# Second block's expert weights: two neighbouring whole rows per partition and transfer, in place of half rows 128 rows apart

## The chip, the cores and the metric

One core of a Trainium2 chip runs the kernel. The metric is the device time of one execution in microseconds (us), as the median of three runs: 2299.51 us before (2298.75 to 2302.57). The profile is of one execution of its own, whose span from the first to the last instruction is 2296.6 us, 2.9 us under that median. Engines are named as in the profile: PE (matrix products), PEld (its weight loads), DVE, ACT and POOL (elementwise work), SP (which issues all DMAs here; SPq is its queue).

## The reference, cut to what matters

The program is two transformer blocks over 256 tokens of width 1024. The second block has two layers: layer 0 is a state-space (SSD) mixer and then experts, over the context's 256 tokens and x's 256; layer 1 is attention and then experts, over x alone. In both, each of 16 experts picks its 32 tokens of a sample by router affinity, and all matrices are 1024 x 1024 in float32:

```
for each sample (layer 0: context and x; layer 1: x)
  h    = rmsnorm(x, norm2_w) * (1 + scale) + shift          # by the sample's modulation
  aff  = softmax(h @ router)                                # [256, 16]
  for each expert e: its 32 tokens of largest aff[:, e]
    g   = h[tokens]                                         # [32, 1024]
    y_e = (silu(g @ w1[e]) * (g @ w3[e])) @ w2[e]
    out[tokens] += aff[tokens, e] * y_e
x += gate * out
```

The experts of one layer have 16 x 3 matrices of 4 MB, 201.3 MB; both layers 402.7 MB of the 601.9 MB that the kernel's DMAs move.

## The kernel before

**Groups.** `choice_run` goes through the experts in groups that fill the 128 partitions with their slots: in layer 0 an expert has S = 64 slots (32 of each sample) and a group has EG = 2 experts, 8 groups; in layer 1 S = 32, EG = 4, 4 groups. `choice_group` multiplies a group's gathered rows with w1, w3 and w2. The rows are the stationary operand, S columns wide, and the weights the moving one, 512 columns at a time, so the experts of a group take different column groups of the PE's array (`tile_position=(0, j * S)`): two of them in layer 0, four in layer 1. The contraction over 1024 has 8 chunks, k = 0 to 7.

**Weights.** `choice_tile` (L1635) loads 2 MB into the next slot of a ring: for all EG experts a part of the chunks and one half n of the columns. Partition p holds row k * 128 + p of chunk k, 512 columns of it, so one contiguous run is 2 KB. A layer-0 tile is two DMAs of 1 MB, a layer-1 tile four of 512 KB. Each layer has 96 tiles, 12 per group in layer 0 and 24 in layer 1. A slot is loaded anew when the products that read it are done. All DMAs stand in SP's one queue in program order, and each waits for the completion of the one eight places before it, so at most eight are under way.

**A group's work.** Per half n of the columns: products with w1 and w3 (L1773), tanh (L1804), two DVE products (L1805, L1806), four transposes (L1809) and a copy into actT (L1810). Then per half n of w2's columns: its product (L1773), y in two parts (ACT L1815, DVE L1816), products with `back` that put the slots' rows back to their tokens (L1822, one pair per sample and 128 tokens), times the gate row (`o`, L1825), added to x or ctx (L1826, on DVE and POOL in turn).

**Before the groups.** `choice` loads the router's weights `wr` (L1652) and scales them. `choice_route` (once for each sample) picks the tokens, and gathers their rows by one-hot products (L1741) whose eight outputs, one per chunk k, are scaled and shifted by `mod_cols` columns into `xg` (DVE L1747 and ACT). In layer 0 the route of the context stands between the two `ssd_out` calls. The rows of scale and shift come from `ada_part` (L1201 to L1227), which also stores the gate rows to DRAM.

**Order.** A scheduler orders each engine's instructions; what limits it are the buffers: PSUM tags "p" and "y" of two banks each, "b" of two, single buffers for `y`, `act` and `o`.

Of the kernel before, what the change touches and what calls it, by code (L numbers as in the profile page):

```python
# [18 lines left out]
F32 = mybir.dt.float32  # L19
# [3 lines left out]
AF = mybir.ActivationFunctionType  # L23
OP = mybir.AluOpType
AX = mybir.AxisListType
PSUM = bass.MemoryType.PSUM
# [52 lines left out]
class Net:  # L79
# [30 lines left out]
    def ring(self):  # L110
        """the next weight slot: the lasting ring and a phase's own in turn"""
# [13 lines left out]
    def weight_slots(self, n, side=None):  # L125
        """n more slots for weights, used in turn with those there are"""
# [38 lines left out]
    def columns(self, groups):  # L165
        """vectors over features, turned into one value per partition"""
# [31 lines left out]
    def load_more(self):  # L198
# [4 lines left out]
        # vectors laid out in every partition  # L203
# [25 lines left out]
    def rstd(self, ss, n, width):  # L229
        """(ss / width + EPS) ** -0.5 for [P, n]"""  # L230
# [16 lines left out]
    def norm_rows(self, xs, A4, rs=None):  # L247
        """rows scaled to unit mean square (no gain): one tile per 128 rows"""
# [13 lines left out]
    def norm_halves(self, xs, tile_, rs=None):  # L262
        """the same in tiles of 128 rows' halves; row tile i's chunk k"""
# [19 lines left out]
    def to_features(self, rows, g, hT, t0=0):  # L283
        """hT[:, k, t0:] = gain * transposed rows"""
# [17 lines left out]
    def rope(self, o, x, cg, sg, tmp, twice=None):  # L302
        """o = x * cg + swapped halves of x * sg; [P, 2, heads, d] with tables [P, 2, d]"""
# [14 lines left out]
    def twice(self, o, x, y, op):  # L318
        """o [P, 2, heads, 2, d]: x op y, twice"""
# [4 lines left out]
    def head_rms(self, x, sq, width):  # L324
        """x [P, 2, heads, width] scaled by its heads' rstd; sq a scratch of its shape"""
# [37 lines left out]
    def gained(self, g, d0, d, step, name):  # L363
        """tables of rope with the gain g of its dims in it"""
# [29 lines left out]
    def attend(self, PT, L, v_of, o_ps, shared):  # L394
        """o_ps [P = (parity, 64), heads / 2, P] from weights L [P, heads, nk]"""
# [89 lines left out]
    def wpairs(self, how, pieces, K, c):  # L485
        """a weight in pairs of its K chunks of 128 rows: [P, 2, c] each"""
# [14 lines left out]
    def split_w(self, how, w):  # L501
        """a pair of a weight's chunks, split: for each chunk its hi and lo"""
# [10 lines left out]
    def lin3(self, how, w, hT):  # L513
        """rows of h times w: one PSUM tile per 128 rows"""
# [9 lines left out]
    def feat3(self, how, w, hT, done):  # L524
        """w^T h, feature-major, two chunks of 128 outputs per PSUM tile: done(chunk, psum)"""
# [11 lines left out]
    def mixer(self, keep, tile_, pool):  # L537
# [23 lines left out]
        # indexer  # L561
# [11 lines left out]
        # latent projections  # L573
# [8 lines left out]
        # queries of the attention over the chosen keys  # L582
# [56 lines left out]
        # gates: tanh of half the logits  # L639
# [8 lines left out]
        # the merge, feature-major: 2 * merged  # L648
# [37 lines left out]
    def index_mask(self, i, s):  # L686
        """0 for the 64 highest scores among the keys that a query sees, NEG for the others"""
# [9 lines left out]
    def latent_heads(self, h0, cT, kpe, tile_, M):  # L697
        """queries, keys (turned) and values of four heads"""
# [66 lines left out]
    def padded_keys(self, tile_, k, cT, sT, tag):  # L765
        """one key head, turned: kT[:, 0] has it in partitions 0:64, kT[:, 1] in 64:128"""
# [14 lines left out]
    def pairs_T(self, A4, q):  # L781
        """[P, 2, 2n heads, 64] -> [P = (parity, 64), n, T]"""
# [13 lines left out]
    def memory_keys(self, keep, M, G):  # L796
        """two pieces of work that wait for nothing: the memory's keys (turned) and values"""
# [43 lines left out]
    def memory_read(self, keep, pool):  # L841
# [3 lines left out]
        # queries, feature-major; the norm's gain is in their weights, its rstd with their own in the logits  # L845
# [76 lines left out]
    def raw_features(self, x, junk, put):  # L922
        """both 128 rows of x, turned: put(where, psum); the rstd of their norm"""
# [15 lines left out]
    CAP = 64  # L939

    def group_moe(self, pool, tile_, late):
# [20 lines left out]
        # group: softmax, first of the largest  # L962
# [19 lines left out]
        # experts of the group: the two largest of affinity + bias  # L982
# [22 lines left out]
        # place of a token in its expert's queue  # L1005
# [5 lines left out]
        # 1000 for a token that isn't there  # L1011
# [15 lines left out]
        # the context's rows will be normalised next  # L1027
# [9 lines left out]
    def group_weights(self, what):  # L1037
        """of a pair of experts half of the rows of gate and up, or all of down"""
# [15 lines left out]
    def down_half(self, late, pr, n):  # L1054
        """half of the columns of a pair of experts' down"""
# [6 lines left out]
    def group_round(self, r, ahead, tile_, late, hi, lo, pos, comb):  # L1062
        """tokens whose place in their expert's queue is in CAP * r + [0, CAP)"""
# [104 lines left out]
    def ada_setup(self):  # L1168
# [9 lines left out]
        self.gates = [self.dp.tile([2, 2, D], F32, name=f"gates{l}") for l in range(2)]  # L1178
        self.ada_done = [0, 0]
        self.ada_rows = {}  # L1180

    def ada_step(self, l, n=1):
        """n 48ths of layer l's modulation: each from 128 of the features a sixth of its columns"""
# [8 lines left out]
    def ada_part(self, l):  # L1192
# [32 lines left out]
        if g % 3 == 2:  # L1225
            for r in range(2):
                nc.sync.dma_start(self.gates[l][g // 3, r].rearrange("(j c) -> j c", j=4), rows[r::32, :])  # L1227
# [7 lines left out]
    def mod_cols(self, l, which, r):  # L1235
        """per feature: norm_w * (1 + scale), shift"""
# [7 lines left out]
    def to_features_mod(self, rows, m, sh, hT, t0, tmp=None):  # L1244
        """hT[:, k, t0:] = m * transposed rows + sh; with tmp, hT is a pair of which the sum is that"""
# [22 lines left out]
    def split(self, hi, lo, x, eng=None):  # L1268
        """x = hi + lo, each in float32r"""
# [3 lines left out]
    def mm3(self, p, L, R, start, stop, **kw):  # L1273
        """p += L^T R of split operands (all but the product of the two small parts)"""
# [42 lines left out]
    def ssd_steps(self, tile_, tmp_, A4, hT):  # L1317
        """step sizes and the cumulative sums of the decays; directions and heads over the partitions"""
# [41 lines left out]
        # from here on each of a direction's heads in four of the partitions  # L1360
# [10 lines left out]
        for d in range(2):  # L1371
# [11 lines left out]
            # moving side: cumulative sums of a quarter of the heads  # L1383
# [13 lines left out]
            # stationary side  # L1397
# [13 lines left out]
            # weights of the context's tokens in the state it leaves  # L1411
# [10 lines left out]
            # sums from x's first (or last) token on  # L1422
# [13 lines left out]
    def ssd_project(self, g, pt_, xt_, hT):  # L1436
        """a group's four heads, B and C, all convolved, and the gate; feature-major"""
# [59 lines left out]
    def ssd_group(self, g, xs, BT, CT, zz, tile_, last=None):  # L1497
# [22 lines left out]
        for q in range(2):  # L1520
# [30 lines left out]
        # the context's final states, and what they give x's tokens  # L1551
# [37 lines left out]
    def ssd_out(self, q, tile_):  # L1589
        """the context's tokens (q = 0) or x's"""  # L1590
# [32 lines left out]
    def ssd_rstd(self):  # L1623
        """of the gated rows, from their squares' sums by partition"""
# [10 lines left out]
    def choice_tile(self, nm, l, e0, EG, q, n):  # L1635
# [472 lines left out]
```

## Time and profile before

| | before |
| --- | --- |
| device time, median of 3 | 2299.51 us |
| profiled execution, span | 2296.6 us |
| PE busy | 1981.3 us, 86% |
| DVE, ACT, POOL busy | 42%, 28%, 20% |
| DMA queue q1 | 601.86 MB in 339294 packets, 73.7% of 16 engines |
| matmuls of the experts (L1773), all three forms of 512 columns in the page | 772 us busy |
| last expert weights landed | 2281.17 us |

The page's slices (40 of 57.4 us) show how full each stage is; the chain of waits shows what ended last. PE's busy time counts records that overlap only once, and its share says nothing of which engine a stage waits for: that is read from the waits of the stage.

### The profile page before, as it was taken

How to read it: one execution, taken by the hardware profiler on the slowest of the kernel's cores; microseconds unless marked ns; L12 is line 12 of the kernel's file. 1: busy time of each engine (PE TensorE's matmuls, PEld its weight loads, DVE VectorE, ACT ScalarE, POOL GpSimd, SP SyncE). 2: the span in 40 equal slices, each digit the busy share in tenths (PEclk: the TensorE clock that was granted, in tenths of full speed). 3: DMA queues.
4: the chain of work that ended last, by engine and by line, in shares of the span. 5: the costliest groups of instructions: out<-in, count | busy, mean ns of one | idle time of the engine just before them, and what ended most of it. 6: DMA issues, size and time to landing. Idle time of an engine off the chain costs nothing. (4 is left out here: it accounts for less than half of the span.)

```text
span 2296.6 us, 24819 instructions
## 1 busy us (share of the span) xinstructions
PE 1981.3 (86%) x9384; PEld 1019.8 (44%) x9384; DVE 966.7 (42%) x1675; ACT 637.2 (28%) x1174; POOL 449.2 (20%) x487
## 2 busy tenths in 40 slices
PE   8889878889999999898898888887988788888886
PEld 7667633366776677565332222222755311111111
DVE  6875532268776677665312222223675210100101
ACT  6454422254554455443100000002453000000000
POOL 4430110032242232511101011112652000000000
PEclk9999989989999999999999999999999799999999
DMA  7554849823332322474999999998349899999997
GB/s 235 186 189 142 286 143 346 287 79 111 120 117 95 110 83 84 150 245 174 363 386 387 386 386 387 387 387 331 149 165 329 299 386 387 386 387 387 387 387 280
DMA packets 339421, 603.53 MB, mean 263 GB/s; under 512 B 23611, under 2 KB 97118, under 8 KB 339294
## 3 DMA queue, kind: packets, MB, share of 16 engines
q1 hardware_dynamic: 339294, 601.86, 73.7%
q8 instruction: 76, 1.25, 0.2%
q14 instruction: 51, 0.42, 0.1%
HBM read 597.05 MB, written 4.75 MB: 262 GB/s over the span
## 5 line engine op out<-in xcount | busy, mean ns | idle before, releaser
L1773 PE MATMUL ps<-w,xg 128*64 128x512 f32 (+1 forms) x2048 | 506.1, 611 | 95.2 <-DMA w<-in_moe_w_dram 95.1
L1773 PEld LDWEIGHTS ps<-w,xg 128*64 128x64 f32 (+1 forms) x2048 | 128.1, 124 | 445.6 <-DMA w<-in_moe_w_dram 267.3
L1826 POOL TENSOR_TENSOR x<-x,o 128x512 f32<-128x512 f32 x24 | 39.2, 1635 | 695.1 <-DVE o L1825 695.1
L1276 PE MATMUL ps<-hT,ws 128*128 128x512 f32 x384 | 162.3, 423 | 4.1 <-DVE ada L1215 4.1
L1773 PE MATMUL ps<-w,ctx 128*32 128x512 f32 x512 | 139.5, 608 | 25.6 <-DMA w<-in_moe_w_dram 25.6
L1278 PE MATMUL ps<-hT,ws 128*128 128x512 f32 x384 | 156.1, 406 | 0.0
L1277 PE MATMUL ps<-hT,ws 128*128 128x512 f32 x384 | 155.8, 406 | 0.0
L1773 PE MATMUL ps<-w,actT 128*64 128x512 f32 x512 | 126.7, 599 | 10.7 <-DMA w<-in_moe_w_dram 9.8
L1805 DVE SCALAR_TENSOR_TENSOR act<-act,ps 128x512 f32<-128x512 f32 x24 | 16.5, 687 | 252.6 <-ACT act L1804 252.6
L1806 DVE TENSOR_TENSOR act<-act,ps 128x512 f32<-128x512 f32 x24 | 16.5, 688 | 250.4 <-PE ps L1773 249.7
L1816 DVE SCALAR_TENSOR_TENSOR y<-ps,s,y 128x512 fp32r<-128x512 f32 x24 | 18.0, 750 | 227.7 <-ACT y L1815 227.7
L1481 DVE SCALAR_TENSOR_TENSOR conv<-pad,cols,conv 128x512 f32<-128x512 f32 x124 | 103.6, 836 | 2.4 <-ACT conv L1474 0.2
L1815 ACT ACTIVATE y<-ps,s 128x512 fp32r<-128x512 f32 x24 | 16.5, 687 | 290.1 <-PE ps L1773 271.8
L1276 PEld LDWEIGHTS ps<-hT,ws 128*128 128x128 f32 x384 | 74.3, 193 | 24.5 <-DVE ada L1215 5.3
L1773 PEld LDWEIGHTS ps<-w,ctx 128*32 128x32 f32 x512 | 25.4, 109 | 130.4 <-DMA w<-in_moe_w_dram 102.2
L1278 PEld LDWEIGHTS ps<-hT,ws 128*128 128x128 f32 x384 | 73.9, 192 | 17.4 <-issue 0.4
L1277 PEld LDWEIGHTS ps<-hT,ws 128*128 128x128 f32 x384 | 74.0, 193 | 16.2 <-issue 0.4
L1804 ACT ACTIVATE act<-ps 128x512 f32<-128x512 f32 x24 | 14.3, 597 | 234.6 <-PE ps L1773 232.9
L1773 PEld LDWEIGHTS ps<-w,actT 128*64 128x64 f32 x512 | 37.6, 136 | 79.9 <-issue 61.9
L1271 DVE TENSOR_TENSOR ws<-wr,ws 128x1024 fp32r<-128x1024 f32 x48 | 61.8, 1290 | 26.2 <-ACT ws L1270 17.9
L1822 PE MATMUL ps<-y,back 128*128 128x512 f32 x160 | 58.2, 450 | 16.6 <-ACT y L1815 7.5
L1271 DVE TENSOR_TENSOR ws<-w,ws 128x1024 fp32r<-128x1024 f32 x46 | 61.3, 1338 | 21.8 <-ACT ws L1270 21.6
(632 smaller groups left out, 3754.3 us busy)
## 6 DMA issues: line engine op xcount, KB each, us to landing
w<-in_moe_w_dram SPq DMA_DIRECT2D x192, 1024.0 KB
w<-in_moe_w_dram SPq DMA_DIRECT2D x384, 512.0 KB
adaw<-in_ada_w_dram SPq DMA_DIRECT2D x34, 512.0 KB
w<-in_moe_w_up_dram SPq DMA_DIRECT2D x32, 512.0 KB
w<-in_moe_w_gate_dram SPq DMA_DIRECT2D x32, 512.0 KB
w<-in_moe_w_down_dram SPq DMA_DIRECT2D x16, 1024.0 KB
wr<-in_ssd_in_w_dram SPq DMA_DIRECT2D x16, 1024.0 KB
w<-in_ssd_out_w_dram SPq DMA_DIRECT2D x32, 512.0 KB
```

Of the source, the lines that this page charges most:

```text
L1271: (eng or self.nc.vector).tensor_tensor(lo, x, hi.bitcast(F32), op=OP.subtract)
L1276: t.matmul(p, lhsT=L[0], rhs=R[0], start=start, stop=False, **kw)
L1277: t.matmul(p, lhsT=L[0], rhs=R[1], start=False, stop=False, **kw)
L1278: t.matmul(p, lhsT=L[1], rhs=R[0], start=False, stop=stop, **kw)
L1481: nc.vector.scalar_tensor_tensor(seq(cv), pad[:, :, j:j + 256], tap(j), seq(cv), op0=OP.mult, op1=OP.add)
L1773: nc.tensor.matmul(p[j * S:(j + 1) * S], lhsT=x(k, j), rhs=w[:, j, kk], start=(k == 0), stop=(k == 7), tile_position=(0, j * S))
L1805: nc.vector.scalar_tensor_tensor(act, act, 1.0, pg[0], op0=OP.add, op1=OP.mult)
L1806: nc.vector.tensor_tensor(act, act, pg[1], op=OP.mult)
L1815: nc.scalar.activation(y[:, 0], p, AF.Copy, scale=ws)
L1816: nc.vector.scalar_tensor_tensor(y[:, 1], p, ws, y[:, 0].bitcast(F32), op0=OP.mult, op1=OP.subtract)
L1822: nc.tensor.matmul(q, lhsT=back[:, (2 * s + i) * P:(2 * s + i + 1) * P], rhs=y[:, v], start=(v == 0), stop=(v == 1))
L1826: (nc.gpsimd if i else nc.vector).tensor_tensor(xx[:, i, c], xx[:, i, c], o, op=OP.add)
```

## The change

A tile is now two experts, two chunks and all 1024 columns. The contraction's chunks are dealt out by steps of eight: chunk k is the rows k, 8 + k, 16 + k and so on, so partition p has row 8p + k, and the two chunks of a tile are the rows 8p + 2q and 8p + 2q + 1, one run of 8 KB, 32 KB from the next partition's. All tiles are two DMAs of 1 MB, in layer 1 too, where a group's four experts need two tiles for each q. A product then makes both halves of the columns at once, in two PSUM banks; `act` is one tile of 1024 columns, and the transposes take every eighth column of it (L1829), as the gather does of the rows (L1754). So y, the products with `back` (L1840) and the additions of a group all come after the whole of w2.

The columns of scale and shift must follow the same dealing. `choice_cols` (L1645) loads them with three small DMAs of 32-byte runs for each sample, from norm2_w and from rows that `ada_part` now stores to DRAM as well (`shifts`), into what `wr` no longer needs, and one DVE instruction (L1651) joins them. The final norm's row, loaded into `ctx_x[:, 0]`, comes later, since that place now holds actT for every group of layer 1.

```diff
-    def choice_tile(self, nm, l, e0, EG, q, n):
-        K = 8 // EG
-        v = self.ring().rearrange("p (e k c) -> p e k c", e=EG, k=K)
-        for e in range(EG):
-            src = self.a[nm][l, e0 + e, q * K * P:(q + 1) * K * P, n * 512:(n + 1) * 512]
-            self.nc.sync.dma_start(v[:, e], src.rearrange("(k p) c -> p k c", p=P))
+    def choice_tile(self, nm, l, e0, q):
+        v = self.ring().rearrange("p (e k c) -> p e k c", e=2, k=2)
+        for e in range(2):
+            src = self.a[nm][l, e0 + e].rearrange("(p k) c -> p k c", k=8)
+            self.nc.sync.dma_start(v[:, e], src[:, 2 * q:2 * q + 2])
         return v
+
+    def choice_cols(self, l, r, t):
+        nc = self.nc
+        rows = [self.a["norm2_w_2"][l], self.shifts[l][1, r], self.shifts[l][0, r]]
+        for j, src in enumerate(rows):
+            nc.sync.dma_start(t[:, j], src.rearrange("(p k) -> p k", k=8))
+        nc.vector.scalar_tensor_tensor(t[:, 0], t[:, 1], 1.0, t[:, 0], op0=OP.add, op1=OP.mult)
+        return t[:, 0], t[:, 2]
...
-                nc.tensor.matmul(p, lhsT=v[:, i, k * P:(k + 1) * P],
+                nc.tensor.matmul(p, lhsT=v[:, i, k::8],
...
-        def product(p, nm, n, x):
-            for q in range(EG):
-                w = self.choice_tile(nm, l, e0, EG, q, n)
-                for kk in range(K):
-                    k = q * K + kk
-                    for j in range(EG):
-                        nc.tensor.matmul(p[j * S:(j + 1) * S], lhsT=x(k, j), rhs=w[:, j, kk],
-                                         start=(k == 0), stop=(k == 7), tile_position=(0, j * S))
+        def product(nm, x):
+            tag = self.turn("py")
+            ps = [self.ps(tag) for _ in range(2)]
+            for q in range(4):
+                ws = [self.choice_tile(nm, l, e0 + j, q) for j in range(0, EG, 2)]
+                for k in (2 * q, 2 * q + 1):
+                    for n, p in enumerate(ps):
+                        for j in range(EG):
+                            nc.tensor.matmul(p[j * S:(j + 1) * S], lhsT=x(k, j),
+                                             rhs=ws[j // 2][:, j % 2, k % 2, n * 512:(n + 1) * 512],
+                                             start=(k == 0), stop=(k == 7), tile_position=(0, j * S))
+            return ps
...
-                nc.tensor.transpose(t[:, k], act[:, k * P:(k + 1) * P], self.ident)
+                nc.tensor.transpose(t[:, k], whole[:, 4 * n + k::8], self.ident)
```

PE, layer 0, from one group's w3 to its w2, before (`xg` is the gathered rows, `w` a ring tile, `oc` the next group's one-hot columns; 64x512 is one product into 64 partitions):

```order
L1773 MATMUL ps_11976<-w_11977,xg_10330 64x512 x8
L1773 MATMUL ps_11976<-w_11988,xg_10330 64x512 x8
L1773 MATMUL ps_12009<-w_12010,actT_11876 64x512
L1809 MATMUL ps_12003<-const,act_11999 128x128 x4
L1789 MATMUL ps_12120<-const,oc_12110 128x128 x4
L1773 MATMUL ps_12009<-w_12010,actT_11876 64x512 x7
```

The same place now, from the last tile of w3 on:

```order
L1792 MATMUL ps_11956<-w_11991,xg_10336 64x512
L1792 MATMUL ps_11957<-w_11991,xg_10336 64x512
L1792 MATMUL ps_11956<-w_11991,xg_10336 64x512
L1792 MATMUL ps_11957<-w_11991,xg_10336 64x512
L1792 MATMUL ps_11956<-w_11991,xg_10336 64x512 x2
L1792 MATMUL ps_11957<-w_11991,xg_10336 64x512 x2
L1829 MATMUL ps_12004<-const,act_11885 128x128 x4
L1829 MATMUL ps_12010<-const,act_11885 128x128 x4
L1792 MATMUL ps_12016<-w_12018,actT_11884 64x512
```

A tile's eight products now alternate between two PSUM banks; in the first chunk the two that stand next to each other are the two halves of the same expert, that is of one column group. All eight transposes stand together between w3 and w2.

SP, layer 0, in the second half of `ssd_out`'s weights for x's tokens, before (`w` from in_ssd_out_w, `yd` the mixer's stored output, `g` gate rows, in_moe_w_2 the first expert tile):

```order
L1652 DMA wr_10333<-in_moe_router_w_dram 128x8x16
L1232 DMA g_2219_10335<-gates_348 128x1024
L1232 DMA g_2220_10337<-gates_348 128x1024
L1606 DMA w_10584<-in_ssd_out_w_dram 128x2x512
L1641 DMA w_11430<-in_moe_w_2_dram 128x4x512
L1606 DMA w_10602<-in_ssd_out_w_dram 128x2x512
L1598 DMA y_10925<-yd_6654 128x2x256
L1606 DMA w_10626<-in_ssd_out_w_dram 128x2x512
```

And now:

```order
L1662 DMA wr_10339<-in_moe_router_w_dram 128x8x16
L1234 DMA g_2219_10341<-gates_348 128x1024
L1234 DMA g_2220_10343<-gates_348 128x1024
L1608 DMA w_10598<-in_ssd_out_w_dram 128x2x512
L1642 DMA w_11442<-in_moe_w_2_dram 128x2048
L1608 DMA w_10616<-in_ssd_out_w_dram 128x2x512
L1650 DMA wr_10339<-in_norm_w_dram 128x8
L1650 DMA wr_10339<-shifts_350 128x8 x2
L1650 DMA wr_10339<-in_norm_w_dram 128x8
L1650 DMA wr_10339<-shifts_350 128x8 x2
L1608 DMA w_10640<-in_ssd_out_w_dram 128x2x512
```

The six small DMAs of `choice_cols` stand between two weight loads of `ssd_out`.

DVE, layer 1, after attention (`t` is attention's output times the gate row, ctx the transposed rows for the router):

```order
L2034 TENSOR_TENSOR t_14774<-ps_14706,g_14701 128x512
L2034 TENSOR_TENSOR t_14845<-ps_14779,g_14701 128x512
L1651 SCALAR_TENSOR_TENSOR wr_14680<-wr_14680 128x8
L2034 TENSOR_TENSOR t_14848<-ps_14780,g_14701 128x512
L1705 COPY ctx<-ps_14869 128x4x128
```

The joining instruction stands ahead of the last of four such products (L2016 before).

## Rows read from the trace of the kernel before

**Rows 1.** The page: GB/s of 40 slices, then packets.

```profile
GB/s 235 186 189 142 286 143 346 287 79 111 120 117 95 110 83 84 150 245 174 363 386 387 386 386 387 387 387 331 149 165 329 299 386 387 386 387 387 387 387 280
DMA packets 339421, 603.53 MB, mean 263 GB/s; under 512 B 23611, under 2 KB 97118, under 8 KB 339294
```

**Rows 2.** Windows: length, busy by engine, PEclk, DMA share, GB/s.

```profile
1245.00:1505.00 260.00, 215.38 (x876) 72.14 (x874) 56.78 (x102) 17.80 (x32) 25.21 (x19) 0.99 1.05 386
2000.00:2200.00 200.00, 168.61 (x620) 32.52 (x619) 15.92 (x24) 6.59 (x13) 6.60 (x4) 1.00 1.05 387
```

**Rows 3.** Chain that ended last, layer 1: start, us, what.

```profile
1742.12 9.37 DMA wr<-in_moe_router_w_dram
...
1797.90 9.38 DMA w<-in_moe_w_dram
...
2062.11 10.82 DMA w<-in_moe_w_dram
...
2281.17 1.92 PE ps L1773 x10
```

**Rows 4.** DMA view of 335:340, 395:400, 1300:1500 and 1645:1650.

```profile
DMA packets 1730, 1.76 MB, mean 351 GB/s; under 512 B 54, under 2 KB 1718, under 8 KB 1729
...
DMA packets 572, 2.02 MB, mean 404 GB/s; under 512 B 27, under 2 KB 96, under 8 KB 572
...
DMA packets 38879, 77.30 MB, mean 387 GB/s; under 512 B 1181, under 2 KB 1181, under 8 KB 38871
...
DMA packets 519, 2.07 MB, mean 414 GB/s; under 512 B 15, under 2 KB 15, under 8 KB 518
```

**Rows 5.** PE's waits in 1245:1505: total us, times, longest.

```profile
PE ps L1773 <- DMA w<-in_moe_w_dram: 32.4, 24, 1.6
PE ps L1809 <- DVE act L1806: 5.1, 8, 0.8
PE ps L1822 <- DVE act L1825: 4.4, 8, 0.6
PE ps L1822 <- ACT y L1815: 2.3, 4, 0.6
```

**Rows 6.** PE's timeline, layer 0: start, us, what, idle before.

```profile
1356.82 3.85 PE L1773 MATMUL ps<-w,xg 128*64 128x512 f32 x16 [1.64 <-DMA w<-in_moe_w_dram]
...
1370.47 0.61 PE L1773 MATMUL ps<-w,actT 128*64 128x512 f32 x1
1370.72 0.59 PE L1773 MATMUL ps<-w,xg 128*64 128x512 f32 x1
```

**Rows 7.** PE's timeline, layer 1.

```profile
1791.79 1.92 PE L1773 MATMUL ps<-w,xg 128*32 128x512 f32 x16
```

**Rows 8.** Timeline at the end of layer 0's experts.

```profile
1589.96 0.69 ACT L1815 ACTIVATE y<-ps,s 128x512 fp32r<-128x512 f32 x1 [0.78 <-PE ps L1773]
1590.68 0.75 DVE L1816 SCALAR_TENSOR_TENSOR y<-ps,s,y 128x512 fp32r<-128x512 f32 x1 [3.61 <-ACT y L1815]
...
1595.86 1.64 POOL L1826 TENSOR_TENSOR ctx<-ctx,o 128x512 f32<-128x512 f32 x1 [0.81 <-DVE o L1825]
```

**Rows 9.** Timeline at the kernel's end.

```profile
2283.18 0.69 ACT L1815 ACTIVATE y<-ps,s 128x512 fp32r<-128x512 f32 x1 [16.00 <-PE ps L1773]
2289.19 1.28 DVE L2024 SCALAR_TENSOR_TENSOR x<-x,s,ctx 128x1024 f32<-128x1024 f32 x1 [0.74 <-POOL s L235]
```

**Rows 10.** SP's timeline around `choice`, layer 0.

```profile
970.41 6.72 SPq L1606 DMA_DIRECT2D w<-in_ssd_out_w_dram  x2
```

**Rows 11.** DVE's timeline around `choice`, layer 1.

```profile
1751.51 0.39 DVE L1659 TENSOR_TENSOR mw<-wr,mod 128x128 f32<-128x128 f32 x1 [8.99 <-DMA wr<-in_moe_router_w_dram]
...
1766.84 0.69 DVE L2016 TENSOR_TENSOR t<-ps,g 128x512 f32<-128x512 f32 x1 [4.75 <-PE ps L1278]
```

**Rows 12.** Chain that ended last, at layer 1's gather.

```profile
1793.71 1.12 PE ps L1741 x4
```

**Rows 13.** The page's groups: weight loads of 128 columns (busy, mean ns, idle before).

```profile
L1276 PEld LDWEIGHTS ps<-hT,ws 128*128 128x128 f32 x384 | 74.3, 193 | 24.5 <-DVE ada L1215 5.3
```

More of the change, by code (lines that the diff above doesn't have):

```diff
@@ L1178, in ada_setup @@
         self.gates = [self.dp.tile([2, 2, D], F32, name=f"gates{l}") for l in range(2)]
+        self.shifts = [self.dp.tile([2, 2, D], F32, name=f"shifts{l}") for l in range(2)]
         self.ada_done = [0, 0]
@@ L1224, in ada_part @@
             nc.vector.tensor_copy(o, tv[:, :, :, r].rearrange("p b j -> p j b"))
-        if g % 3 == 2:
+        if g >= 2:
+            to = self.gates[l][g // 3] if g % 3 == 2 else self.shifts[l][g - 3]
             for r in range(2):
-                nc.sync.dma_start(self.gates[l][g // 3, r].rearrange("(j c) -> j c", j=4), rows[r::32, :])
+                nc.sync.dma_start(to[r].rearrange("(j c) -> j c", j=4), rows[r::32, :])
     def gate_row(self, pool, l, gi, r, tag, bufs, tile_=None):
@@ L1666, in choice @@
             o["cw"].append(cw)
+        left = wr.rearrange("p k e -> p (k e)")
+        for s, (_, r) in enumerate(samples):
+            o["cols"].append(self.choice_cols(l, r, left[:, 24 * s:24 * s + 24].rearrange("p (j k) -> p j k", j=3)))
         return o
@@ L1687, in choice_route @@
         aff, pos, xg, mw, cw = o["aff"], o["pos"], o["xg"], o["mw"][s], o["cw"][s]
-        m, sh = self.mod_cols(l, 1, r)
+        m, sh = o["cols"][s]
         hi, lo = tmp_([P, 2, D], "hi", 1, F32R), tmp_([P, 2, D], "lo", 1, F32R)
@@ L1752, in choice_run @@
         for grp in range(16 * S // P):
-            t = actT[:, grp % 2].rearrange("p (k c) -> p k c", k=8) if actT is not None else tile_([P, 8, P], "actT", 2)
-            self.choice_group(o["l"], grp, P // S, S, o["samples"], o["xg"], o["aff"], o["pos"], o["gr"], t, tile_)
+            if actT is None:
+                t, act = tile_([P, 8, P], "actT", 1), tile_([P, D], "act", 1)
+            else:
+                t, act = actT[:, 0].rearrange("p (k c) -> p k c", k=8), actT[:, 1]
+            self.choice_group(o["l"], grp, P // S, S, o["samples"], o["xg"], o["aff"], o["pos"], o["gr"], t, act, tile_)
     def turn(self, tags):
@@ L1759, in turn, with choice_group @@
         return tags[self.turns % len(tags)]
-    def choice_group(self, l, grp, EG, S, samples, xg, aff, pos, gr, actT, tile_):
+    def choice_group(self, l, grp, EG, S, samples, xg, aff, pos, gr, actT, whole, tile_):
         nc = self.nc
+        acts = [whole[:, n * 512:(n + 1) * 512] for n in range(2)]
         NS = len(samples)
-        e0, K = grp * EG, 8 // EG
-        def product(p, nm, n, x):
-            for q in range(EG):
-                w = self.choice_tile(nm, l, e0, EG, q, n)
-                for kk in range(K):
-                    k = q * K + kk
-                    for j in range(EG):
-                        nc.tensor.matmul(p[j * S:(j + 1) * S], lhsT=x(k, j), rhs=w[:, j, kk],
-                                         start=(k == 0), stop=(k == 7), tile_position=(0, j * S))
+        e0 = grp * EG
+        def product(nm, x):
[10 more added lines that the diff above has]
+            return ps
         oc = tile_([P, NS, 2, EG, NS, 32], "oc", 1)
@@ L1791, in choice_group @@
         ws = self.st([P, 1])
-        junk = tile_([P, 512], "act", 1)[:, :nt * P]
+        junk = tile_([P, 512], "o", 2)[:, :nt * P]
         nc.scalar.activation(junk, t, AF.Copy, scale=0.5, accum_out=ws)
@@ L1795, in choice_group @@
         nc.vector.tensor_scalar(back, junk, 0.0, None, op0=OP.is_gt)
-        for n in range(2):
-            pg, tag = [], self.turn("py")
-            for nm in ("moe_w1_2", "moe_w3_2"):
-                p = self.ps(tag)
-                product(p, nm, n, lambda k, j: xg[:, k, e0 + j].rearrange("p s c -> p (s c)"))
-                pg.append(p)
-            act = tile_([P, 512], "act", 1)
-            nc.scalar.activation(act, pg[0], AF.Tanh, scale=0.5)
-            nc.vector.scalar_tensor_tensor(act, act, 1.0, pg[0], op0=OP.add, op1=OP.mult)
-            nc.vector.tensor_tensor(act, act, pg[1], op=OP.mult)
+        rows = lambda k, j: xg[:, k, e0 + j].rearrange("p s c -> p (s c)")
+        for act, p in zip(acts, product("moe_w1_2", rows)):
+            nc.scalar.activation(act, p, AF.Tanh, scale=0.5)
+            nc.vector.scalar_tensor_tensor(act, act, 1.0, p, op0=OP.add, op1=OP.mult)
+        for n, p in enumerate(product("moe_w3_2", rows)):
+            act = acts[n]
+            nc.vector.tensor_tensor(act, act, p, op=OP.mult)
+        for n in range(2):
             t = self.ps("t").rearrange("p (k c) -> p k c", k=4)
             for k in range(4):
-                nc.tensor.transpose(t[:, k], act[:, k * P:(k + 1) * P], self.ident)
+                nc.tensor.transpose(t[:, k], whole[:, 4 * n + k::8], self.ident)
             nc.scalar.activation(actT[:, 4 * n:4 * n + 4], t, AF.Copy)
-        for n in range(2):
-            p = self.ps(self.turn("py"))
-            product(p, "moe_w2_2", n, lambda k, j: actT[:, k, j * S:(j + 1) * S])
+        for n, p in enumerate(product("moe_w2_2", lambda k, j: actT[:, k, j * S:(j + 1) * S])):
             y = tile_([P, 2, 512], "y", 1, F32R)
@@ L1823, in choice_group @@
                                          start=(v == 0), stop=(v == 1))
-                    o = tile_([P, 512], ("act", "o")[i], 1)
+                    o = tile_([P, 512], "o", 2)
                     nc.vector.tensor_tensor(o, q, gr[s][:, c], op=OP.mult)
```

2 lines of the change are left out of this document (1 added, 1 removed).

## The prediction, made before the changed kernel ran

> **What bounds the kernel now.** I read the page's slices first, then the windows of the two expert stages, the chain of waits, and PE's waits and timeline in layer 0. In the page, two stretches hold 386 to 387 GB/s [rows 1], the experts of the two layers: seven slices after one of 363, which begins at 1091 us, and seven of the last eight. At 363 of 387 the first stretch is full from about 1095 us. In layer 1 the chain is weights alone: from 1797.90 it goes from tile pair to tile pair in steps of 10.82 us, until the last has landed at 2281.17 [rows 3]; 483.3 us at 5.41 us per tile are 89 tiles, the other 7 having been loaded ahead. PE makes a layer-1 tile's sixteen records in 1.92 us [rows 7], so nothing but the transfers counts there. In layer 0 PE comes closer: a tile takes it 3.85 us [rows 6] and the group is more than products. The window 1245 to 1505 is four groups of 65 us; PE is busy 215.4 us of it [rows 2], and of its waits 32.4 us are for weights, 11.8 us for DVE and ACT [rows 5]. So PE needs (215.4 + 11.8) / 4 = 56.8 us per group where the transfers take 65. From 1095 to the end of layer 0's last product, about 1589.9 [rows 8], less its 3.8 us, 491 us hold 90 tiles at 5.42 us.
>
> **What a longer run is worth.** Before shows runs of three lengths in stretches in which the queue is full [rows 4]. Counting out the small packets, the packets are 1 KB at 351 GB/s, 2 KB at 387 and 4 KB at 404 to 414 GB/s (1 KB: first block's gate and up; 4 KB: its down and the modulation's weights). With 16 engines side by side, one packet takes its engine 46.7 ns, 84.7 ns, and 158 to 162 ns. So the second KB costs 38 ns, and each of the two after it 37 to 39; what is left over per packet is about 9 ns. For 8 KB no row exists. From the 4 KB rows on, four more KB at 37 to 39 ns give 305 to 317 ns, an estimate of 413 to 429 GB/s. I take 420, a tile in 4.99 us. Bounds: 404, the lower 4 KB row (5.19 us), as if runs over 4 KB gained nothing; 429 (4.89 us). Below lies only what the runs' distance may do, a rival.
>
> Layer 1: 89 x (5.41 - 4.99) = 37 us less (20 to 46). Layer 0: 90 x (5.42 - 4.99) = 39 us less (21 to 48), if PE keeps up. A group's transfers would take 12 x 4.99 = 59.9 us against PE's 56.8. That need grows: before, a half's transposes waited 0.6 us for DVE [rows 5] and could stand behind a product of the next half; now all eight need both halves, the second 0.7 us multiplication comes on top, and no product of w2 can precede them. I add 1.5 us: 58.3 of 59.9. The ring lets transfers run on through such a pause, but with 1.6 us of slack some pauses will show: 0.5 us per group, 4 us. Layer 0 gives 35 us.
>
> **What the change adds.**
> - End of layer 0: from y's ACT at 1589.96 to POOL's last addition at 1597.50 [rows 8] half of the columns go through y, `back`, `o` and the addition. Now both halves do, behind one `y`: four more `o` and two more additions on DVE (0.69 us each), and a second y of 0.69 + 0.75 us. 5 us (4 to 6); attention waits for it.
> - End of layer 1: likewise two more `o` and one more addition (2.1 us) and a second y (1.4 us); and the last weights now complete two tiles' products, some 1.9 us instead of the last part of one. 5 us (4 to 6). The final norm's 512 KB are now issued after the last w2 product, not 15 tiles earlier; they are needed at L2024, 6 us after the first y [rows 9], and 512 KB at 404 GB/s take 1.3 us: nothing, or 2 us if their start is slow.
> - `choice_cols`, layer 0: six small DMAs take places among the eight. The next load of `ssd_out`, issued at 970.41 and now behind them [rows 10], must wait until the first expert tile's 1 MB lands. Without a row for the delay: 0 if PE's work ahead lasts, 7 us, the length of that issue row, if not. I take 3.
> - `choice_cols`, layer 1: `wr` is on the chain, 9.37 us behind 4 MB of weights [rows 3]; the same 4 MB stand ahead of it now, so it is not later. The columns follow, behind up to 4 MB more (10 us), from 1752.5 on: landed about 1763 to 1765. DVE needs them ahead of its product at 1766.84 [rows 11]: hidden, with 2 us to spare; 0, or 3 if late, as four copies for the router stand behind it on DVE.
> - Stationary operands with steps of eight columns (gather, transposes) appear in no row. A plain load of 128 columns takes 193 ns [rows 13], the gather's products come every 280 ns [rows 12]: a load of the old length hides, one of twice that shows by 0.1 us, 32 times in a sample, 3 us. Faster it can't get, since the data are the same. I take 1 us.
> - The eight small stores of `shifts` wait for DVE in SP's queue just as the gate rows do, in stages whose slices show 80 to 330 GB/s [rows 1]: nothing; 1 us each layer without that cover.
>
> Sum against the profiled execution: 2296.6 - 37 - 35 + 5 + 5 + 3 + 1 = 2238.6; its span lies 2.9 us under the median, so 2241 us.
>
> **Rivals.**
> 1. PE's column groups lose their overlap and layer 0 becomes PE's (slower). Now two products of the same column group stand next to each other in each tile's first chunk. If products start strictly as they stand, with two records each, the sixteen records of a tile fill ten places of 0.47 us (16 records in 3.8 us, two at a time) where eight did: 4.7 us per tile. A group needs 12 x 0.9 = 11 us more, 69.6 us instead of 58.3, and 4.6 more than the 65 of before: over 7.5 groups +35 us instead of -35, and 2311 in all. It turns slower once a layer-0 tile costs PE 4.6 us. Against it: layer 1's sixteen records in 1.92 us [rows 7] are four column groups at once, in an order that puts each product's two records together, so PE looks some records ahead; and at 1370.47 the first product of w2 starts before the last record of w3 [rows 6], which stands ahead of it in PE's order. The Trainium skill (TensorE: Matmul & The Clock Gate, Part 3, The mechanism) says that matmuls start and end strictly in program order; by that rule this rival would hold and the sum be 2311. The rows disagree at 1370.47, so I leave it one chance in twelve.
> 2. Nothing gained beyond 4 KB: packets may be cut there, so that the change does only half of what it says. At 404 GB/s both layers give 41 us, layer 0 without PE's pauses: 2299.5 - 41 + 14 = 2273; at 414, with 62 us, 2252. For it: no packet of the page shows an 8 KB run; against it: the cost per KB was even up to 4 KB.
> 3. The full estimate and no pauses: 429 GB/s gives 94 us; less 10 us of costs, 2216. It needs PE at 58.3 us per group to hide under 58.7.
> 4. The runs' distance of 32 KB: 128 partitions read at equal steps of a power of two, which no weights here do. It turns slower below 393 GB/s, where 179 tiles give just 14 us. Its price, by the lowest full-queue row, 351: 179 x 0.56 + 14 = 114 us, 2414. The Trainium skill (DMA: Bandwidth & Descriptors, Latency and other measured facts) reports loads with such steps at 207 GB/s for 512 KB and 214 undisturbed, and much less from 2 MB on; it has none of 32 KB. Taking those 3% off 420 would give 407 GB/s and about 2266 in place of 2241. No run here shows it.
>
> **How the numbers follow.** The forecast with its own range of 2225 to 2257: 0.54. Rival 2 and gains down to 2290: 0.20. Rival 3 and better than 2225: 0.10. Rival 1: 0.08. Rival 4 at its worse end: 0.04. The rest, 0.04, is a gain that the tails and PE's pauses eat. A difference of 0.2%, 4.6 us, is about what can be told from none. Faster 0.84, same 0.04, slower 0.12. The range from 2214 to 2290 leaves out the two slower rivals, no change, and the edge of rival 3.
>
> **What would show it.** The GB/s of the two stretches: 420 confirms the step, 404 to 414 is rival 2, under 393 rival 4. Packets in them fall to a quarter if runs stay whole. In layer 1 the chain is still weights, 10.0 us per pair. In a window of four groups of layer 0, PE's waits for weights shrink from 32 us to some 10; a tile's sixteen records stay near 3.8 us, or go to 4.7 in rival 1. The `o` rows at both ends number twice as many after the last product. The prediction is wrong if layer 0's stretch is not some 30 us shorter while layer 1's is, or if weights wait longer around `choice_cols` than 7 us.

## The result: 2218.34 us, 0.9647 of before

The changed kernel took 2218.34 us as the median of four runs (2217.77 to 2219.81), beside 2299.79 us for the kernel before: a ratio of 0.9647, 95% interval [0.9634, 0.9661]. That is 81 us less, where 59 had been forecast. The time lies in the range of 2214 to 2290, but near its lower end, and not in the forecast's own range of 2225 to 2257. Later, beside other kernels, the same file gave 0.9644 [0.9626, 0.9663]. The profiled execution has a span of 2218.0 us, 78.6 less than before.

The page of the changed kernel, GB/s of its 40 slices (55.5 us each) and its packets, which answer to [rows 1]:

```profile
GB/s 240 180 199 132 280 101 346 320 126 102 118 115 124 116 85 67 111 183 222 277 420 419 420 419 420 420 419 365 173 156 297 291 421 420 420 421 421 420 422 280
DMA packets 190251, 603.57 MB, mean 272 GB/s; under 512 B 21867, under 2 KB 95406, under 8 KB 140974
```

The bytes are the same. Packets fell from 339421 to 190251; 49277 are now of 8 KB or more, where before there were 127. So the runs stay whole. Both stretches that held 387 GB/s hold 420. Its windows, which answer to [rows 2] (length, busy by engine, granted clock, DMA share, GB/s):

```profile
1245.00:1505.00 260.00, 248.33 (x955) 93.06 (x953) 64.02 (x115) 19.44 (x36) 34.36 (x23) 1.00 1.01 420
...
1980.00:2180.00 200.00, 166.74 (x666) 40.51 (x665) 11.37 (x17) 6.41 (x12) 3.24 (x2) 1.00 1.01 421
```

In layer 1 the chain is still weights, now in steps of four tiles (a group's w needs two tiles for each q, and the view joins two such steps):

```profile
1762.85 15.75 DMA w<-in_moe_w_dram
1778.62 19.92 DMA w<-in_moe_w_dram
...
2178.60 19.85 DMA w<-in_moe_w_dram
2198.49 2.78 PE ps L1792 x18
```

19.9 us for four tiles are 9.95 per pair, against 10.82 in [rows 3]; the forecast had said 10.0. PE's waits in layer 0, which answer to [rows 5] (here in 1245 to 1485, 240 us, about four of the shorter groups):

```profile
PE ps L1792 <- DMA w<-in_moe_w_dram: 7.0, 13, 0.6
PE ps L1829 <- DVE act L1824: 3.1, 4, 0.8
PE ps L1792 <- ACT actT L1830: 1.0, 4, 0.2
PE ps L1840 <- ACT y L1833: 0.3, 1, 0.3
```

PE now waits 7 us for weights where it waited 32. The way in which the prediction worked out PE's need, (240 - 7.0) / 4, gives 58.2 us per group, close to its 58.3. But this is not PE's need: where the two halves of a tile land one after the other, its records are drawn out. Two earlier groups, in which PE waits for no weights at all, show less (start and end of the first by its transposes):

```profile
1122.73 1.16 PE L1829 MATMUL ps<-const,act 128*128 128x128 f32 x8 [0.78 <-DVE act L1824]
...
1174.62 1.16 PE L1829 MATMUL ps<-const,act 128*128 128x128 f32 x8 [0.78 <-DVE act L1824]
...
1229.56 1.16 PE L1829 MATMUL ps<-const,act 128*128 128x128 f32 x8 [0.78 <-DVE act L1824]
```

They take 51.9 and 54.9 us, where the transfers of a group take 59.9.

Where the time went, by what starts at each point in the two traces (us):

| from, to | before | after | change |
| --- | --- | --- | --- |
| start, first expert product of layer 0 | 1080.0 | 1081.6 | +1.6 |
| to y of the last group's last product | 510.0 | 463.9 | -46.1 |
| to attention's norm (DVE L259) | 8.1 | 14.2 | +6.1 |
| to the router's columns of layer 1 (L1659, now L1669) | 153.5 | 149.9 | -3.6 |
| to the one-hot rows of its gather (L1736, now L1749) | 33.8 | 34.7 | +0.9 |
| to the last weights landed | 495.9 | 454.3 | -41.6 |
| to the end | 15.4 | 19.5 | +4.1 |

"After" counts y from its first half, which starts before the second half's products end. The 1.6 us of the first row can't be told from none: in two executions of the changed kernel the first expert product starts at 1081.6 and 1079.4 us.

### The profile page after: what moved, and what is told of

Its sections match the earlier page's. It is cut to its first block, busy times and chain, and to the rows that moved or that the text cites. A ratio compares the mean times of both kernels' runs of the same rounds, so it can differ in the third digit from the quotient of the medians.

```text
span 2218.0 us, 24627 instructions
## 1 busy us (share of the span) xinstructions
PE 1973.0 (89%) x9363; PEld 1056.2 (48%) x9384; DVE 963.6 (43%) x1675; ACT 636.1 (29%) x1174; POOL 453.0 (20%) x487
## 2 busy tenths in 40 slices
DMA packets 190251, 603.57 MB, mean 272 GB/s; under 512 B 21867, under 2 KB 95406, under 8 KB 140974
## 5 line engine op out<-in xcount | busy, mean ns | idle before, releaser
L1792 PE MATMUL ps<-w,xg 128*64 128x512 f32 (+1 forms) x2048 | 496.6, 602 | 52.8 <-DMA w<-in_moe_w_dram 52.7
L1792 PEld LDWEIGHTS ps<-w,xg 128*64 128x64 f32 (+1 forms) x2048 | 142.5, 123 | 374.2 <-issue 242.5
L1792 PE MATMUL ps<-w,ctx 128*32 128x512 f32 x512 | 128.2, 599 | 23.9 <-DMA w<-in_moe_w_dram 22.9
L1792 PEld LDWEIGHTS ps<-w,actT 128*64 128x64 f32 x512 | 45.5, 136 | 79.2 <-issue 63.4
L1843 DVE TENSOR_TENSOR o<-ps,g 128x512 f32<-128x512 f32 x80 | 51.7, 686 | 62.1 <-PE ps L1840 61.5
L1544 POOL TENSOR_TENSOR seg<-seg,seg 128x512 f32<-128x512 f32 x32 | 45.4, 1418 | 128.4 <-ACT seg L1542 128.4
L1542 ACT ACTIVATE seg<-ps 128x512 f32<-128x512 f32 x96 | 55.2, 599 | 53.0 <-PE ps L1540 23.5
L1272 ACT ACTIVATE ws<-w 128x1024 fp32r<-128x1024 f32 x52 | 54.2, 1054 | 43.6 <-PE ps L1280 31.1
```

The costliest lines, as they stand in the source:

```text
L1272: self.nc.scalar.activation(hi, x, AF.Copy)
L1542: nc.scalar.activation(e, p, AF.Exp)
L1544: nc.gpsimd.tensor_tensor(ex[0][0], ex[0][0], ex[1][0], op=OP.add)
L1792: nc.tensor.matmul(p[j * S:(j + 1) * S], lhsT=x(k, j), rhs=ws[j // 2][:, j % 2, k % 2, n * 512:(n + 1) * 512], start=(k == 0), stop=(k == ...
L1843: nc.vector.tensor_tensor(o, q, gr[s][:, c], op=OP.mult)
```

## Experiments

Theory A: the rate of a full queue depends on the length of the contiguous run, and nothing else in the change matters much. Its rivals were that whole rows, or their dealing, or larger DMAs do it; that the distance of 32 KB costs something; and that PE has become layer 0's limit. The first four kernels ran together (before: 2297.5 us), the last four too (before: 2299.03 us).

**Separate rows of 4 KB** (runs4k). The changed kernel with chunks q and q + 4 in a tile:

```diff
-            self.nc.sync.dma_start(v[:, e], src[:, 2 * q:2 * q + 2])
+            self.nc.sync.dma_start(v[:, e], src[:, q::4])
...
-                for k in (2 * q, 2 * q + 1):
+                for k in (q, q + 4):
```

> The changed kernel, but a tile's two chunks are q and q + 4, so that a partition reads two separate rows of 4 KB; the dealing by steps of eight, the 32 KB from partition to partition and the 1 MB per DMA stay. Theory A, the length of the run sets the rate: 404 to 414 GB/s in the expert stages, a tile in 5.07 to 5.19 us where the changed kernel has 4.97, some 185 tiles, so 18 to 41 us slower than the changed kernel: 2236 to 2259. Rival B, it is the whole rows (a tile of 1 MB per expert in complete rows) and not the run: rate stays at 420, 2218.

Measured: 2250.26 us, ratio 0.9795 [0.9779, 0.9812]. A window of layer 0:

```profile
1250.00:1500.00 250.00, 235.24 (x893) 85.80 (x893) 56.52 (x105) 18.06 (x33) 29.58 (x21) 1.00 1.03 409
```

409 GB/s, between the two 4 KB rows of before [rows 4]. Rival B falls: with whole rows and 1 MB per DMA, half the run gives 409 instead of 420 GB/s. The kernel takes back some 34 of the 81 us (0.0148 of before), but not all of it by the rate: 0.135 us for each of 178 tiles are 24 us. The order of the products is not the same. The second chunk of a tile is now q + 4, which the gather delivers later, so the first slot of a layer comes free later: by the packets of the traces, the first new weights start 11.4 us after layer 0's first expert product (7.8 in the changed kernel) and 16.2 us after the one-hot rows of layer 1 (12.0). That is another 8 us.

**Whole rows, chunks of 128 neighbouring rows** (rows128). The dealing of before, with no `choice_cols`, no stores of `shifts` and no operands in steps of eight:

```diff
-            src = self.a[nm][l, e0 + e].rearrange("(p k) c -> p k c", k=8)
+            src = self.a[nm][l, e0 + e].rearrange("(k p) c -> p k c", p=P)
...
-                nc.tensor.matmul(p, lhsT=v[:, i, k::8],
+                nc.tensor.matmul(p, lhsT=v[:, i, k * P:(k + 1) * P],
...
-                nc.tensor.transpose(t[:, k], whole[:, 4 * n + k::8], self.ident)
+                nc.tensor.transpose(t[:, k], whole[:, (4 * n + k) * P:(4 * n + k + 1) * P], self.ident)
```

> Whole rows of 1024 columns as in the changed kernel, but chunk k is again the rows k * 128 + p: runs of 4 KB, the next partition's row right behind it, no choice_cols, no stores of shifts, no operands in steps of eight. Theory A: the same rate as the kernel with separate 4 KB rows, 404 to 414 GB/s; 2236 to 2259, less 0 to 5 for what choice_cols and the strided operands cost. Rival C, the distance of 32 KB costs something: this kernel reads faster than the one with separate 4 KB rows.

Measured: 2244.77 us, 0.9774 [0.9757, 0.979].

```profile
1250.00:1500.00 250.00, 235.82 (x890) 85.87 (x887) 55.98 (x103) 17.91 (x33) 29.46 (x20) 1.00 1.03 409
```

The same 409 GB/s with a distance of 4 KB as with 32 KB: rival C falls, and with it the fourth rival of the prediction for this distance. The time is 5.5 us under the kernel with separate 4 KB rows, and the two intervals overlap. That is no price of the strided operands, the stores and `choice_cols`: here the first new weights start 7.7 us after layer 0's first expert product and 11.7 us after layer 1's one-hot rows, 8 us less in all than in runs4k. What those three cost does not show.

**Halves of rows, 2 KB** (runs2k). Four DMAs of 512 KB per tile, all else as changed:

```diff
-            self.nc.sync.dma_start(v[:, e], src[:, 2 * q:2 * q + 2])
+            for n in range(2):
+                c = slice(n * 512, (n + 1) * 512)
+                self.nc.sync.dma_start(v[:, e, :, c], src[:, 2 * q:2 * q + 2, c])
```

> The changed kernel with each expert's part of a tile loaded as two DMAs of half the columns, 512 KB each in runs of 2 KB; the products and their order stay. Theory A: 387 GB/s, as before the change, 5.42 us per tile, so some 0.45 us x 185 = 83 us slower than the changed kernel: about 2301, within 6 of the kernel before. Rival B: 420 GB/s and 2218.

Measured: 2297.05 us, 0.9994 [0.9983, 1.0005].

```profile
1250.00:1500.00 250.00, 236.03 (x840) 79.45 (x837) 55.32 (x98) 16.28 (x30) 25.41 (x19) 1.00 1.05 386
```

This is the cleanest of the experiments: everything of the change is in it but the run's length and the 1 MB per DMA, and nothing of the gain is left. The size of a DMA is not it: before, layer 0 with 1 MB and layer 1 with 512 KB held 386 and 387 GB/s [rows 2]. What the change adds at the layers' ends and around `choice` is in this time too, but so is a gain that needs no longer run: the first new weights start 8.0 us after layer 0's first expert product, where before it was 13.7 (see below).

**16 KB** (runs16k). A tile is one expert's four neighbouring rows in one DMA:

```diff
-        v = self.ring().rearrange("p (e k c) -> p e k c", e=2, k=2)
...
+        v = self.ring().rearrange("p (k c) -> p k c", k=4)
+        src = self.a[nm][l, e0].rearrange("(p k) c -> p k c", k=8)
+        self.nc.sync.dma_start(v, src[:, 4 * q:4 * q + 4])
...
-            for q in range(4):
-                ws = [self.choice_tile(nm, l, e0 + j, q) for j in range(0, EG, 2)]
-                for k in (2 * q, 2 * q + 1):
+            for q in range(2):
+                ws = [self.choice_tile(nm, l, e0 + j, q) for j in range(EG)]
+                for k in range(4 * q, 4 * q + 4):
```

> A tile is one expert's four neighbouring rows, one DMA of 2 MB with runs of 16 KB; a layer-0 product waits for two tiles, a layer-1 product for four. Theory A, with the fixed part of a packet and the cost per KB of the runs so far: 16 KB in about 614 ns, 427 GB/s, 4.91 us per tile, 0.06 x 185 = 11 us less in transfers; of that up to 8 are given back, since layer 0's PE need of 58.2 us per group is then above 58.9 less its pauses, and the last tiles of both layers complete more products at once: 2208 to 2218. Rival D, the rate has reached its ceiling at 8 KB: 420 GB/s, and the coarser tiles make it slower, 2219 to 2226.

Measured: 2229.95 us, 0.9709 [0.9691, 0.9726]: the rate as theory A has it, the time as neither has it.

```profile
1250.00:1500.00 250.00, 228.11 (x933) 86.62 (x930) 57.52 (x104) 18.05 (x33) 29.37 (x20) 0.98 1.01 427
```

So where did the gain go? The windows in which the ring is full at the start of each layer tell it. The changed kernel:

```profile
1085.00:1095.00 10.00, 10.00 (x40) 4.90 (x40) 0.81 (x1) 1.13 (x2) 0.00 (x0) 1.00 0.54 211
...
1755.00:1765.00 10.00, 10.00 (x65) 4.83 (x62) 1.62 (x2) 0.78 (x1) 0.00 (x0) 1.00 0.88 351
1765.00:1775.00 10.00, 7.84 (x54) 2.37 (x53) 4.50 (x19) 2.34 (x5) 0.00 (x0) 1.00 1.01 422
```

With 16 KB runs throughout:

```profile
1085.00:1095.00 10.00, 10.00 (x38) 4.98 (x38) 0.81 (x1) 1.55 (x2) 0.00 (x0) 1.00 0.00 0
...
1755.00:1765.00 10.00, 10.00 (x66) 4.97 (x63) 0.81 (x1) 1.55 (x2) 0.00 (x0) 1.00 0.00 0
1765.00:1775.00 10.00, 10.00 (x72) 3.66 (x72) 2.56 (x9) 1.19 (x2) 0.00 (x0) 1.00 0.97 390
```

A slot comes free when all chunks in it are used, and the first product of a layer gets its chunks one by one from the gather. With four chunks in a tile the first slot comes free later, and the queue stands empty meanwhile: 211 and 351 GB/s against none, in 10 us each. The first new weights start 6.3 and 6.4 us later than in the changed kernel, which uses up what the rate saves, 11 us by the expectation. From the last weights to the end it is 23.5 us instead of 20.0. The rest of the 12 us between the two kernels' times stays open.

**Is layer 0 still the transfers'?** (halfpe)

```diff
                         for j in range(EG):
+                            if NS == 2 and n and k:
+                                continue
```

> The changed kernel, but in layer 0 the products of the second half of the columns are made for the first chunk only (7/16 of layer 0's expert products are left out; all weights are still loaded). Theory A, layer 0 is still the transfers': from its first expert product to its last 464.6 us become 461 to 464, the rate stays 420 GB/s. Rival P, PE with 58.2 us of need per group against 59.6 already costs layer 0 something: below 458 us.

Measured: 2220.11 us in one run, 2218.3 span. From the first expert product to the end of the last it is 460.8 us in this kernel and 464.7 in the changed one beside it, just below what theory A gave and above rival P's 458. PE's waits in 1245 to 1485:

```profile
PE ps L1794 <- DMA w<-in_moe_w_dram: 46.0, 50, 1.4
PE ps L1843 <- ACT y L1836: 4.2, 5, 0.8
```

PE waits 46 us for weights instead of 7, and the stage is 3.9 us shorter. The last rows of the layer's products, of this kernel and of the changed one beside it, account for 1.7 us of that:

```profile
1541.22 1.93 PE L1794 MATMUL ps<-w,actT 128*64 128x512 f32 x6 [1.44 <-DMA w<-in_moe_w_dram]
...
1540.39 3.65 PE L1792 MATMUL ps<-w,actT 128*64 128x512 f32 x12 [0.59 <-DMA w<-in_moe_w_dram]
```

From the first new weights to these rows it is 451.9 us here and 453.2 there. Rival P falls. The 4 us that I charged for PE's pauses are 1.3 at most.

**The router's weights ahead of the expert tiles, in the kernel before** (before_wr):

```diff
+            self.wr1 = self.cut(slots.enter_context(self.pool("wr1")))([P, 8, 16], "wr1")
+            nc.sync.dma_start(self.wr1, self.a["moe_router_w_2"][1].rearrange("(k p) c -> p k c", p=P))
             with self.pool("att") as ap:
                 oT, ao = self.attention(ap, right)
```

> The kernel before the change, but layer 1's router weights are loaded at the start of attention, not behind the first expert tiles. Theory A, the 3.5 us that the changed kernel saves between attention's norm and the router's columns come from the place of that load in the queue: 2 to 9 us faster than before (DVE waits 9.0 us for it; PE and the attention's output weights may stand behind). Rival: that work waits for attention's output product anyway, within 1 us of before.

Measured: 2295.93 us, 0.9988 [0.9978, 0.9999]: 2.8 us less, which is in theory A's range but hardly clear of nothing. DVE's wait of 9.0 us for `wr` is gone, but from attention's norm to the one-hot rows, the stretch in question, it takes 186.1 us instead of 187.3. The row behind which it now stands:

```profile
1747.24 0.17 DVE L1665 COPY cw<-ps 128x16 f32<-128x16 f32 x1 [4.29 <-PE ps L1664]
1749.82 2.59 DVE L1271 TENSOR_TENSOR ws<-w,ws 128x1024 fp32r<-128x1024 f32 x2 [2.40 <-ACT ws L1270]
```

The chain through `wr` was real, but another stands 1.2 us behind it. So the load's place explains no more than that of the 3.6 us that this stretch gained after the change; the rest, some 2 us, stays open.

**The best of both** (mixed16). 16 KB runs but for the first group's w1 and the last group's w2 of each layer, and layer 0's second y in a buffer that is free by then:

```diff
+            if (nm, grp) not in (("moe_w1_2", 0), ("moe_w2_2", 16 // EG - 1)):
+                for q in range(2):
+                    ws = [self.choice_tile4(nm, l, e0 + j, q) for j in range(EG)]
...
-            y = tile_([P, 2, 512], "y", 1, F32R)
+            y = tile_([P, 2, 512], "act" if n and NS > 1 else "y", 1, F32R)
```

> 16 KB runs (a tile is one expert's four rows) everywhere but in the first group's w1 and the last group's w2 of each layer, which keep the 8 KB tiles of two experts; and layer 0's second y has a buffer of its own. Theory A, the kernel with 16 KB throughout lost its gain where the ring is given free after routing and at the ends: 427 GB/s over some 165 tiles, 0.06 us each, 10 us less than the changed kernel, and 2 more from y: 2204 to 2212. Rival D, the coarser tiles lose it in the middle, in pauses of PE or of the ring: 2216 or more.

Measured: 2210.03 us, 0.9614 [0.9596, 0.9632], beside 2217.73 of the changed kernel in the same batch (after_again): it beats the changed kernel and the one with 16 KB throughout, and the time lies in theory A's range, though the gain is 7.7 us where 12 were expected.

> The changed kernel again, on the chip and beside the runs of the other kernels of this batch: ratio 0.963 to 0.966 to the kernel before.

Measured: 2217.73 us, 0.9644 [0.9626, 0.9663].

Layer 1's start in the kernel with mixed tiles:

```profile
1745.00:1755.00 10.00, 10.00 (x66) 4.64 (x69) 1.62 (x2) 0.91 (x2) 0.00 (x0) 1.00 0.37 133
1755.00:1765.00 10.00, 10.00 (x78) 3.95 (x70) 2.56 (x9) 1.43 (x2) 0.00 (x0) 1.00 1.01 430
```

The queue no longer stands empty there. Layer 0 gave less than its rate: the last w2 of the layer runs without a wait for weights (row below, 64 records in 14.33 us), so its end is PE's now.

```profile
1529.39 14.33 PE L1807 MATMUL ps<-w,actT 128*64 128x512 f32 x64 [0.24 <-ACT actT L1845]
```

## Why the prediction was right, and where it was short

**The run's length sets the rate: right, in mechanism and in size.** Four lengths are now measured in the same place. At 387, 409, 420 and 427 GB/s over 16 engines, packets of 2, 4, 8 and 16 KB take 84.7, 160, 312 and 614 ns. From 2 KB on each KB costs 37.7 to 38.0 ns, and some 9 to 11 ns are left per packet, about what the 1 KB and 2 KB rows had said. The 420 GB/s that I took were 420.

**The savings were mis-sized, by about 16 us.** Forecast were 37 and 35 us, measured are 41.6 and 46.1. In layer 0 the 39 us for the rate were right: from the first new weights to the start of the last tile's last products it is 492.5 us before and 453.2 now, 39.3 less for the same 90 tiles. What failed there:
- PE's pauses, 4 us: 1.3 at most (halfpe). The step behind them was PE's need of 58.3 us per group; groups without a wait for weights take 51.9 and 54.9. Between w3's last product and w2's first PE makes no expert product for 2.2 us (1345.49 to 1347.67), and the ring carries the transfers over it: the stretch holds 420 GB/s all the same.
- The start of the layer, which the sum left out. In the kernel before, a layer-0 tile holds four chunks, and the first slot comes free only when the gather has delivered the fourth; now it holds two. The first expert product starts at 1080.0 before and at 1081.6 now, the first new weights start 13.7 and 7.8 us after it: 5.9 us, by the chunks in a tile and not by the run (8.0 us in runs2k, with two chunks and runs of 2 KB). It is the price that runs16k paid again (14.1 us). Before, then now:

```profile
1090.00:1092.00 2.00, 2.00 (x10) 0.87 (x8) 0.00 (x0) 0.31 (x1) 0.00 (x0) 1.00 0.00 0
1092.00:1094.00 2.00, 2.00 (x12) 0.57 (x8) 0.00 (x0) 0.47 (x1) 0.00 (x0) 1.00 0.24 25
1094.00:1096.00 2.00, 2.00 (x10) 0.96 (x10) 0.46 (x1) 0.00 (x0) 0.00 (x0) 1.00 0.74 281
...
1086.00:1088.00 2.00, 2.00 (x11) 0.75 (x10) 0.00 (x0) 0.78 (x1) 0.00 (x0) 1.00 0.00 0
1088.00:1090.00 2.00, 2.00 (x10) 1.25 (x8) 0.23 (x1) 0.00 (x0) 0.00 (x0) 1.00 0.34 57
1090.00:1092.00 2.00, 2.00 (x12) 0.71 (x10) 0.58 (x1) 0.00 (x0) 0.00 (x0) 1.00 0.91 373
```

- The last products: y starts 2.9 us after the last tile's last products begin (1542.62 to 1545.51) instead of 3.8 (1586.20 to 1589.96), as the halves of the last tile's products end one after the other: 1 us.

In layer 1, 88 tiles follow the first new weights in both kernels, and 0.87 us per pair make 38 us. Two terms were left out. The final norm's 512 KB, which stood among these weights, now follow them: 1.3 us. And before, the queue held only 320, 335, 280 and 375 GB/s in the steps of 2 us from 1798 to 1806, when it started again: 1.2 us. Some 1 us stays open. Of the 88 us that the two layers gained, 78 are thus the rate's and 6 come of the chunks in a tile.

That the time lies in the stated range is in part luck: the sum was 22 us too high, and the range reached so low to cover rival 3, which did not come.

**The additions.** The end of layer 0 cost 6.1 us, or 5 counted from the last product's start, for 5; the kernel's end 4.1 for 5; `choice_cols` of layer 0 1.6 for 3, within what two executions differ by; the gather and the route of layer 1 0.9 for 1. `choice_cols` of layer 1 is hidden, but not as comfortably as said of the columns' landing; DVE waits for them by 1.1 us and then again for PE, which covers it:

```profile
1720.21 0.69 DVE L2034 TENSOR_TENSOR t<-ps,g 128x512 f32<-128x512 f32 x1 [1.97 <-PE ps L1280]
1721.97 0.33 DVE L1651 SCALAR_TENSOR_TENSOR wr<-wr 128x8 f32<-128x8 f32 x1 [1.06 <-DMA wr<-shifts]
1725.66 0.69 DVE L2034 TENSOR_TENSOR t<-ps,g 128x512 f32<-128x512 f32 x1 [3.36 <-PE ps L1280]
```

**The attention stretch, forecast unchanged, gained 3.6 us.** I had said that `wr` is not later. It is earlier: before, its issue at 1742.12 waited until the third 512 KB of the tiles ahead of it, issued at 1735.31, had landed; now it follows the first four 1 MB pieces at 1700.55 without a wait. In before_wr the stretch to the one-hot rows gained 1.2 us by it, with one execution of each kernel.

**Rival 1**, PE's column groups in strict order, did not come. PE's timeline of the changed kernel in layer 0:

```profile
1374.54 1.93 PE L1792 MATMUL ps<-w,xg 128*64 128x512 f32 x4
...
1377.55 14.81 PE L1792 MATMUL ps<-w,xg 128*64 128x512 f32 x64
1392.93 4.42 PE L1792 MATMUL ps<-w,xg 128*64 128x512 f32 x16 [0.57 <-DMA w<-in_moe_w_dram]
```

Where tiles lie ready, 64 records of four tiles take 14.81 us, 3.70 each: two column groups side by side all the way, as before, although the order has pairs of one group in it. Where they don't, a tile takes 4.42 us, and four records alone 1.93: those of the first expert, whose 1 MB lands first. With the strict order of starts and ends that the Trainium skill states (TensorE: Matmul & The Clock Gate, Part 3, The mechanism) the prediction had worked out 4.7 us for a tile that lies ready, an estimate; with 3.70 this trace does not agree with it for products in different column groups.

**Rival 2** would have been the 2250 us of runs4k. **Rival 3** had the time (2216) by the wrong means: no pauses, but 429 GB/s, where 420, the earlier start of layer 0 and a shorter attention stretch made it. **Rival 4** is refuted for 4 KB runs at 32 KB by runs4k and rows128, and with 8 KB runs the 420 GB/s lie on the same line of ns per KB. I had said that no weights here are read at equal steps of a power of two; those of the kernel before are, at 4 KB from partition to partition. The 3% that I had taken from what the Trainium skill (DMA: Bandwidth & Descriptors, Latency and other measured facts) gives for copies at a row pitch of 512 KB do not show here at 32 KB, 409 against 409 GB/s.

## What to carry to other kernels

Where a full DMA queue is the chain, read the packet length first: here a packet costs some 9 to 11 ns and 37.7 to 38.0 ns per KB on its engine, so that whole rows, and neighbouring rows on one partition, gave 6 and 9% more GB/s. Dealing the contraction out by steps is a way to get them without a change of the data. The price is granularity: a tile with more chunks frees its slot later, so the first and last product of a stage should keep the small ones. It cuts both ways: with two chunks instead of four, layer 0 of this kernel won 5.9 us at its start that have nothing to do with the run.

## What I had not expected

- The rate goes on rising beyond 8 KB: 427 GB/s at 16 KB.
- Weight loads with a step of eight columns: the gather's (128 columns) take 312 to 346 ns, where the median was 188 before; as expected that shows only in part: four gather products went from 1.12 us [rows 12] to between 1.28 and 1.30. The transposes' went from 140 to 193 ns and cost nothing that shows: the transposes themselves take 276 ns where they took 273.
- With 16 KB runs PE's granted clock fell in layer 1: 0.88 to 0.91 in windows of 100 us, and 0.85 to 0.90 in the kernel with mixed tiles, where the changed kernel has 1.00. These are means of stretches at the full level (2.4 GHz) and at the half (1.2 GHz). PE waits up to 3 us at a time for four tiles there, where the changed kernel's longest wait from 1800 to 2180 is 1.8 us. A row of the kernel with mixed tiles:

```profile
2000.00:2100.00 100.00, 70.28 (x341) 17.72 (x339) 7.25 (x12) 2.94 (x6) 3.24 (x2) 0.90 1.01 427
```
